# A hybrid encoder layer on one core: mLSTM exponents made from a broadcast row part and a bias column, the row preparation in steps

## The chip, the core and the metric

The kernel runs on one core of a Trainium2 chip. The metric is the device time of one execution in microseconds, compared by medians of several runs. A core has a matrix engine (TensorE, PE in the profile, with PEld for its weight loads), VectorE (DVE), ScalarE (ACT), GpSimd (POOL), and SyncE (SP), which here issues all transfers between the chip's memory and SBUF. Matmul results go to PSUM. Each engine works off its own instructions in order and waits for others by semaphores.

## The reference

The layer takes x (2048 tokens x 1024), 256 memory tokens and the weights. It normalises x and makes one wide projection of it, from which three mixers run: an mLSTM in both directions, an attention in a two-dimensional neighbourhood, and a cross-attention into the memory tokens. Their outputs are projected, weighted by sigmoid gates, summed, projected again and added to x; an MLP with squared ReLU follows. The change touches the mLSTM alone (4 heads, queries and keys of 64, values of 128). Its chunk step in the reference, cut to what matters:

```python
b = jnp.cumsum(lf, axis=-1)
d_log = where(tril, b[..., :, None] - b[..., None, :] + ig[..., None, :], -inf)
inter = b + m_st[..., None]
m_t = maximum(inter, max(d_log, axis=-1))
s = einsum('bhtd,bhsd->bhts', q, k) * exp(d_log - m_t[..., None])
w_inter = exp(inter - m_t)
num = einsum('bhts,bhsv->bhtv', s, v) + w_inter[..., None] * einsum('bhvd,bhtd->bhtv', c_st, q)
den = sum(s, axis=-1) + w_inter * einsum('bhd,bhtd->bht', n_st, q)
h = num / maximum(abs(den), exp(-m_t))[..., None]
```

The exponent of a pair (query t, key s) is a sum of two parts: a_s = ig_s - b_s belongs to the key, r_t = b_t - m_t to the query. In the kernel a tile of exponents has the keys s on the 128 partitions and (head, query t) on the free axis, so that r is the row part and a the column part.

## The kernel before

Three phases follow each other: the projections and the two attentions; the mLSTM, with matmuls of the late gates between its own; then the merge, the output projection and the MLP. Every large product is three fp32r matmuls of split operands, high and low halves (lines L232 to L234). The order on TensorE is written by hand: a generator per stream of work is advanced by one step ("tick") after every six gate matmuls, and what it emits stands there in TensorE's order. The other engines are ordered by a scheduler; for them the place in the program sets the priority.

Phase 2 (`phase_2`) goes from some 950 to 1350 us. `late_gates` gives the 48 groups of 24 gate matmuls with four ticks in each. Its `ml_stream` waits START_2 = 20 ticks and then gives one chunk of 128 tokens per slot of four ticks, forward and backward directions in turn, 32 chunks in all. The table `when` says in which tick of a slot the chunks of the same direction take their next step: an entry (age, ...) is the chunk that began `age` slots of its direction ago.

At the first chunk of each quarter of 512 tokens `ml_block` prepares the rows of its direction: it loads the logs of both gates on four partitions (one a head), scans them to b and m, makes a and r, splits both into halves for an fp32r product (tiles `at` and `rp`), makes w = exp(r + m of the chunk before), stores w, and transposes m by four small matmuls (L773), of which ACT makes exp(-m) (`em`).

`ml_chunk` is the generator of one chunk. Its steps: the loads, and on POOL the tile `rd`, the rows r spread on a block diagonal; then one matmul of `at` and `rd` (L810), which gives a_s + r_t for all heads in PSUM, and the exponential `de` on ACT (L812), masked by POOL; then the scores (L822) or their saved copy `sk`, and `pt` = scores x `de` on DVE; then the transposes of the keys (L839), with `sk` saved by ACT for the direction that passes this chunk later (L832), and the scaled keys `kw`; then the numerator (L863, L866); then the state update (L872, L878), the denominator and `h`. In the later half of a direction's chunks `h` of the other direction (`hf`) is added (L894), squares are summed on ACT (L897), one step later `h` is scaled (L901), and one more step later transposed (L905), split into `hm` and stored. In PSUM this phase has two buffers of 128 x 512 fp32 for the gates (tag mm), four for the numerators (pn), and a ring of two (mx) for everything else, L810 and the transposes included. The gates' results are taken from PSUM by ACT (L600, tile `ev`). A weight comes by DMA as `wr` and is split by ACT (L176) and DVE (L177). `PAD` is the size in bytes of a partition of an unused tile ahead of the tiles of phases 2 and 3 (L251); the large tile X of phase 3 lies behind it.

Of the kernel before, what the change touches and what calls it, by code (L numbers as in the profile page):

```python
# [22 lines left out]
S = 2048  # L23
TB = 512
LOW, LATER, LATER_A, SOON = 100, 60, 60, 40
TICKS_2, START_2 = 4, 20
PAD = 192
EV = {1: 2, 2: 2, 3: 8}
XT = 2
PREP_V = 2  # L30
# [50 lines left out]
class Body:  # L81
# [206 lines left out]
    def scratch(self):  # L288
        d = lambda name, shape, dt=F32: self.p_d.tile(shape, dt, name=name)
        self.scr = dict(  # L290
            qk=d("s_qk", [128, 4, S]),
            v=[d(f"s_v{b}", [TB, 512]) for b in range(NB)],
            og=[d(f"s_o{b}", [TB, 512]) for b in range(NB)],
            gate=[d(f"s_g{b}", [24, 128, TB]) for b in range(NB)],
            qs=d("s_qs", [128, 8, 2, 2, 2, 128]),
            ks=d("s_ks", [128, 2, 2, S]),
            vna=d("s_vna", [2, ROWS, 40, 256]),
            hf=[d(f"s_hf{c}", [128, 512]) for c in range(S // 128)],
            sk=[d(f"s_sk{c}", [128, 6, 128]) for c in range(S // 128)],
            hna=d("s_hna", [128, 2, 2, S]),  # L300
            hmem=d("s_hmem", [128, 2, 2, S]),
            ig=d("s_ig", [8, S]),
            fg=d("s_fg", [8, S]),
            lf=d("s_lf", [8, S]),
            w=[[d(f"s_w{i}{b}", [4, TB]) for b in range(NB)] for i in range(2)],
            hm=[d(f"s_hm{b}", [128, 2, 4, TB]) for b in range(NB)],
            hT={b: d(f"s_hT{b}", [128, 2, 8, TB]) for b in SPILL},
            x2=[d(f"s_x2{b}", [TB, D]) for b in range(NB)],

            a=[[d(f"s_a{i}{q}", [128, 3, 2, TB]) for q in range(FF // 512)] for i in range(NB // 2)],
            s=[[d(f"s_s{i}{q}", [128, 4, 2, TB]) for q in range(FF // 512)] for i in range(NB // 2)],
            t=[d(f"s_t{q}", [128, 2, 2, 2, 512]) for q in range(FF // 512)],
        )
# [308 lines left out]
    def ml_stream(self):  # L624


        for _ in range(START_2):
            yield
        dirs = [list(range(16)), list(range(15, -1, -1))]
        live = [[], []]  # L630
        when = {0: [(2, 0)], 1: [(1, 1), (2, 1), (3, 0)], 2: [(1, 2)], 3: [(3, 0), (1, 3), (0, 1)]}
        d = 0
        while any(dirs) or any(live[0]) or any(live[1]):
            c = dirs[d].pop(0) if dirs[d] else None
            if c is not None and c % 4 == (0, 3)[d]:
# [39 lines left out]
    def ml_consts(self):  # L675
        nc, p = self.nc, self.p_a
        t = lambda name, shape, dt=F32: p.tile(shape, dt, name=name)


        self.reset = t("reset", [36, TB])  # L680
        nc.vector.memset(self.reset, 1.0)
        nc.vector.memset(self.reset.rearrange("p (c t) -> p c t", t=128)[:, :, 0:1], 0.0)

        self.bd = t("bd", [36, 4, 128])
        nc.vector.memset(self.bd, 0.0)
        for d in range(2):
            nc.gpsimd.affine_select(out=self.bd, in_=self.bd, compare_op=ALU.not_equal, fill=1.0, base=-32 * d,
                                    pattern=[[-1, 4], [0, 128]], channel_multiplier=1)


        self.at, self.rd, self.rp = {}, {}, {}
        for d in range(2):
            for i in range(2):
# [3 lines left out]
                for x in (at, rd, rp):  # L697
                    nc.gpsimd.memset(x.bitcast(F32), 0.0)
                for k in range(2):
                    nc.vector.tensor_copy(rd[32 * k:32 * k + 4], self.bd[32 * k:32 * k + 4])  # L700
                    nc.vector.tensor_scalar(at[64 + 32 * k:68 + 32 * k], self.reset[32 * k:32 * k + 4], 0.0, 1.0, ALU.mult, ALU.add)
        self.carry = t("carry", [36, 1])
        nc.vector.memset(self.carry, NEG)
        self.packs = []
# [5 lines left out]
        nc.vector.tensor_scalar(self.gml, raw, 0.5, None, ALU.mult)  # L710
# [27 lines left out]
    def ml_block(self, d, b):  # L738

        nc = self.nc  # L740
        n = b if d == 0 else 3 - b
        hs = slice(32 * d, 32 * d + 4)
        if d == 0:
            self.packs.append({x: self.row("r_" + x, (36, TB + (x == "m")), bufs=1) for x in "ifbmw"})
        P = {x: y[hs] for x, y in self.packs[n].items()}
        ig, lf, bs, m, w = (P[x] for x in "ifbmw")
        nc.sync.dma_start(ig, self.scr["ig"][4 * d:4 * d + 4, b * TB:(b + 1) * TB])
        nc.sync.dma_start(lf, self.scr["lf"][4 * d:4 * d + 4, b * TB:(b + 1) * TB])
        rev = (lambda x: x[:, ::-1]) if d else (lambda x: x)
        nc.vector.tensor_tensor_scan(rev(bs), self.reset[hs], rev(lf), 0.0, ALU.mult, ALU.add)  # L750
        cm, ce = (m[:, 1:], m[:, 0:1]) if d == 0 else (m[:, :TB], m[:, TB:])
        carry = self.carry[hs]
        nc.vector.tensor_copy(ce, carry)
        nc.vector.tensor_tensor_scan(rev(cm), rev(lf), rev(ig), ce, ALU.add, ALU.max)
        nc.vector.tensor_copy(carry, m[:, TB:] if d == 0 else m[:, 0:1])
        lo = slice(32 - 32 * d, 36 - 32 * d)
        at, rp = self.at[d, n % 2], self.rp[d, n % 2]
        a, r = ig, bs
        nc.vector.tensor_tensor(a, ig, bs, ALU.subtract)
        nc.scalar.activation(at[hs], a, AF.Copy)  # L760
        nc.vector.tensor_tensor(at[lo], a, at[hs].bitcast(F32), ALU.subtract)
        nc.vector.tensor_tensor(r, bs, cm, ALU.subtract)
        nc.scalar.activation(rp[hs].bitcast(F32R), r, AF.Copy)
        nc.vector.tensor_tensor(rp[lo], r, rp[hs], ALU.subtract)
        ms = (m[:, 0:TB] if d == 0 else m[:, 1:]).rearrange("p (c t) -> p c t", t=128)
        ms = ms[:, :, 0:1] if d == 0 else ms[:, :, 127:128]
        nc.vector.tensor_tensor(w.rearrange("p (c t) -> p c t", t=128), r.rearrange("p (c t) -> p c t", t=128),
                                ms.to_broadcast([4, 4, 128]), ALU.add)
        nc.scalar.activation(w, w, AF.Exp)
        self.store(self.scr["w"][d][b], w)  # L770
        p = self.ps("mx", (128, 4, 128))
        for c in range(4):
            nc.tensor.transpose(p[:, c, 0:4], cm[:, c * 128:(c + 1) * 128], self.ident[hs, hs])  # L773
        em = self.row(f"r_em{d}", (128, 4, 4))
        nc.scalar.activation(em, p[:, :, 0:4], AF.Exp, scale=-1.0)
        self.rows[d, b] = dict(at=at, rp=rp, em=em)

    def ml_chunk(self, d, c):

# [30 lines left out]
        nc.tensor.matmul(pd, R["at"][:, cs], rd, start=True, stop=True)  # L810
        de = self.t(f"de{d}", [128, 4, 128], 1)
        nc.scalar.activation(de, pd, AF.Exp)  # L812
# [765 lines left out]
```

## Time and profile before

| | |
|---|---|
| median of 3 runs | 2993.33 us (2991.52 to 2995.25) |
| the profiled execution | 2998.03 us, of which the span is 2996.3 us |
| TensorE busy | 2929.4 us, 98% of the span |
| VectorE busy | 2066.5 us, 69% |
| ScalarE busy | 1195.8 us, 40% |
| GpSimd busy | 268.8 us, 9% |
| transfers | 632.97 MB, 211 GB/s on average |

Rows of groups read: line, engine, operation, output<-inputs, count, then the least, median and largest duration in ns or the total in us. Rows of waits read: the waiting engine, its tile and line, "<-", the releaser; then the total in us, how many there were, and the longest. In a stretch of time a row has its length, the busy time of each engine with the number of instructions, the granted clock of TensorE as a share of full speed (PEclk), the busy share of the DMA engines and what they moved. A row of time has start, duration, engine, line, operation and tiles, and in brackets the idle time before it with its releaser.

### The profile page before, as it was taken

The numbers are of one execution on the slowest core, as the hardware profiler recorded it, in microseconds if no ns is written. First come the engines' busy times: TensorE is split into PE (matmuls) and PEld (weight loads), VectorE is DVE, ScalarE is ACT, GpSimd is POOL, SyncE is SP. The second block draws the span as 40 slices with busy tenths as digits, with TensorE's granted clock in tenths as the row PEclk, the third lists the DMA queues.
The fourth block names the chain that finished last, engine by engine and source line by source line (L and its number), as shares of the span: only waits on it lengthen the run. The fifth ranks groups of instructions, "written<-read, shape, count | busy, mean of one in ns | idle before, by whom it ended". The sixth has DMA issues, their size and how long they took to land.

```text
span 2996.3 us, 41916 instructions
## 1 busy us (share of the span) xinstructions
PE 2929.4 (98%) x15028; PEld 2375.1 (79%) x15028; DVE 2066.5 (69%) x3523; ACT 1195.8 (40%) x2198; POOL 268.8 (9%) x423
## 2 busy tenths in 40 slices
PE   8999999999989899999999999999999999999999
PEld 6888888778777677778888888888778888888887
DVE  6676864476654766765688878666675987885665
ACT  6465654355543333342243333533312433334331
POOL 4121200021001323420000000000000000000000
PEclk9999999999999999999999999999999999999999
DMA  8786877876998667788444445766863444466554
GB/s 276 222 275 200 242 231 246 275 215 203 289 283 267 199 202 236 247 275 306 141 132 161 144 149 178 256 195 218 280 209 119 148 151 146 142 223 226 191 185 165
DMA packets 341712, 632.97 MB, mean 211 GB/s; under 512 B 29344, under 2 KB 151008, under 8 KB 341504
## 3 DMA queue, kind: packets, MB, share of 16 engines
q1 hardware_dynamic: 341504, 630.30, 65.5%
q8 instruction: 118, 1.93, 0.3%
q14 instruction: 90, 0.74, 0.1%
HBM read 453.63 MB, written 176.55 MB: 210 GB/s over the span
## 4 chain that ended last, share of the span: by engine, by line
PE 55%; DVE 2%; DMA 2%; issue 1%; ACT 0%; POOL 0%; SPq 0%; DVEq 0%; ACTq 0%; POOLq 0%
PE mm L232 18%; PE mm L233 18%; PE mm L234 18%; PE mm L1341 0%; DMA wr<-in_w_units_dram 0%; DMA hf<-s_hf 0%; DVE h L901 0%; DMA og<-s_o 0%; DVE ev L1497 0%; DVE acc L1490 0%; ACT hf L897 0%; POOL rs L325 0%; DMA X<-s_a 0%; DVE ws L177 0%; DVE h L889 0%
## 5 line engine op out<-in xcount | busy, mean ns | idle before, releaser
L232 PE MATMUL mm<-X,ws 128*128 128x512 f32 x1152 | 455.7, 396 | 0.0
L234 PE MATMUL mm<-X,ws 128*128 128x512 f32 x1152 | 455.4, 395 | 0.0
L233 PE MATMUL mm<-X,ws 128*128 128x512 f32 x1152 | 455.4, 395 | 0.0
L232 PE MATMUL mm<-hT,ws 128*128 128x512 f32 x896 | 375.0, 419 | 8.2 <-DMA hT<-s_hT 4.4
L177 DVE TENSOR_TENSOR ws<-wr,ws 128x1024 fp32r<-128x1024 f32 (+1 forms) x212 | 264.5, 1254 | 136.2 <-ACT ws L176 132.6
L234 PE MATMUL mm<-hT,ws 128*128 128x512 f32 x896 | 353.2, 394 | 0.0
L233 PE MATMUL mm<-hT,ws 128*128 128x512 f32 x896 | 353.2, 394 | 0.0
L233 PE MATMUL mm<-X 128*128 128x512 f32 x896 | 349.6, 390 | 3.4 <-DVE X L1464 3.4
L234 PE MATMUL mm<-X 128*128 128x512 f32 x896 | 349.3, 390 | 0.5 <-DVE X L1464 0.5
L232 PE MATMUL mm<-X 128*128 128x512 f32 x896 | 349.3, 390 | 0.0
L1463 ACT ACTIVATE X<-X 128x1024 fp32r<-128x1024 f32 x176 | 186.6, 1062 | 324.7 <-DMA X<-s_t 115.7
L1464 DVE TENSOR_TENSOR X<-X 128x1024 fp32r<-128x1024 f32 x176 | 214.6, 1224 | 136.7 <-ACT X L1463 135.8
L176 ACT ACTIVATE ws<-wr 128x1024 fp32r<-128x1024 f32 (+1 forms) x212 | 223.4, 1058 | 163.8 <-PE mm L234 88.9
L232 PE MATMUL mm<-ws,hT 128*128 128x512 f32 (+2 forms) x704 | 259.8, 369 | 2.7 <-ACT zif L524 1.8
L234 PEld LDWEIGHTS mm<-X,ws 128*128 128x128 f32 x1152 | 216.4, 188 | 52.3
L232 PEld LDWEIGHTS mm<-X,ws 128*128 128x128 f32 x1152 | 216.4, 188 | 52.2
L233 PEld LDWEIGHTS mm<-X,ws 128*128 128x128 f32 x1152 | 216.5, 188 | 52.1
L234 PE MATMUL mm<-ws,hT 128*128 128x512 f32 (+2 forms) x704 | 249.6, 355 | 2.0 <-DVE hT L434 2.0
L233 PE MATMUL mm<-ws,hT 128*128 128x512 f32 (+2 forms) x704 | 248.9, 354 | 0.0
L202 ACT ACTIVATE ws<-wr 128x512 fp32r<-128x512 f32 x224 | 135.1, 629 | 229.8 <-PE mm L234 148.8
L232 PEld LDWEIGHTS mm<-hT,ws 128*128 128x128 f32 x896 | 170.1, 190 | 49.7 <-issue 10.7
L234 PEld LDWEIGHTS mm<-hT,ws 128*128 128x128 f32 x896 | 169.6, 189 | 38.9
(266 smaller groups left out, 4865.8 us busy)
## 6 DMA issues: line engine op xcount, KB each, us to landing
wr<-in_w_units_dram SPq DMA_DIRECT2D x308, 512.0 KB
s_s<-u SPq DMA_DIRECT2D x32, 1024.0 KB
X<-s_s SPq DMA_DIRECT2D x64, 512.0 KB
X<-s_t SPq DMA_DIRECT2D x64, 512.0 KB
s_g<-ev SPq DMA_DIRECT2D x96, 256.0 KB
ev<-s_g SPq DMA_DIRECT2D x96, 256.0 KB
s_a<-u SPq DMA_DIRECT2D x96, 256.0 KB
X<-s_a SPq DMA_DIRECT2D x48, 512.0 KB
```

The costliest lines, as they stand in the source:

```text
L176: nc.scalar.activation(w[:, 0], raw, AF.Copy)
L177: nc.vector.tensor_tensor(w[:, 1], raw, w[:, 0].bitcast(F32), ALU.subtract)
L202: nc.scalar.activation(hi, src, AF.Copy)
L232: mm(out, lhs[0], rhs[0], start=first, stop=False)
L233: mm(out, lhs[0], rhs[1], start=False, stop=False)
L234: mm(out, lhs[1], rhs[0], start=False, stop=last)
L1463: nc.scalar.activation(hi, src, AF.Copy)
L1464: nc.vector.tensor_tensor(lo, src, hi.bitcast(F32), ALU.subtract)
```

## The change

The tiles `bd`, `at`, `rd`, `rp` and the matmul L810 go. `ml_block` becomes `ml_rows`, a generator for both directions of a block together: one step per tick, with the loads four ticks ahead of the first scan. It stores r to a new scratch `s_r`, and transposes the column part a beside m, giving four bias columns per chunk (`ac`). A chunk loads its 4 x 128 row values to all 128 partitions (`rb`, 256 KB), and `de` is made by four activations, exp(rb + ac), one a head. The first preparation begins at tick 8 of the 20 ahead of the first chunk (ROWS_2), the next ones at slots 3, 11 and 19, that is five slots ahead of their first chunk. One set of row tiles (`pack`) serves all four blocks. In `when` the entry (3, 0) of tick 1 moves to tick 0: in the later half that is the step that scales `h` (L901). PAD goes from 192 to 256 bytes.

```diff
-TICKS_2, START_2 = 4, 20
-PAD = 192
+TICKS_2, START_2, ROWS_2 = 4, 20, 8
+PAD = 256
...
+            r=[[d(f"s_r{i}{b}", [4, 4, 128]) for b in range(NB)] for i in range(2)],
...
-        for _ in range(START_2):
+        rows = self.ml_rows(0)
+        for tick in range(START_2):
+            if tick >= ROWS_2:
+                next(rows, None)
             yield
+        slot = 0
...
-        when = {0: [(2, 0)], 1: [(1, 1), (2, 1), (3, 0)], 2: [(1, 2)], 3: [(3, 0), (1, 3), (0, 1)]}
+        when = {0: [(2, 0), (3, 0)], 1: [(1, 1), (2, 1)], 2: [(1, 2)], 3: [(3, 0), (1, 3), (0, 1)]}
...
-            if c is not None and c % 4 == (0, 3)[d]:
-                self.ml_block(d, c // 4)
+
+            if slot % 8 == 3 and slot < 24:
+                rows = self.ml_rows(slot // 8 + 1)
+            slot += 1
...
+                next(rows, None)
                 yield
...
-        self.bd = t("bd", [36, 4, 128])
...
-                at = self.at[d, i] = t(f"at{d}{i}", [100, TB], F32R)
-                rd = self.rd[d, i] = t(f"rd{d}{i}", [100, 4, 128], F32R)
-                rp = self.rp[d, i] = t(f"rp{d}{i}", [36, TB])
...
+        self.pack = [t("r_" + x, [36, TB + 2 * (x == "m")]) for x in "ifbmw"]
+        for x in self.pack:
+            nc.gpsimd.memset(x, 0.0)
...
+    def ml_rows(self, n):
+        nc = self.nc
+        ig, lf, bs, m, w = self.pack
+        cm, a, r = m[:, 1:TB + 1], ig, bs
+        dirs = [(d, n if d == 0 else 3 - n, slice(32 * d, 32 * d + 4)) for d in range(2)]
+        rev = lambda d, x: x[:, ::-1] if d else x
+        for d, b, hs in dirs:
+            for x, name in ((lf, "lf"), (ig, "ig")):
+                nc.sync.dma_start(x[hs], self.scr[name][4 * d:4 * d + 4, b * TB:(b + 1) * TB])
+        for _ in range(4):
+            yield
+        for d, _, hs in dirs:
+            nc.vector.tensor_tensor_scan(rev(d, bs[hs]), self.reset[hs], rev(d, lf[hs]), 0.0, ALU.mult, ALU.add)
+            yield
+        for d, _, hs in dirs:
+            ce = m[hs, 0:1] if d == 0 else m[hs, TB + 1:TB + 2]
+            carry = self.carry[hs]
+            nc.vector.tensor_copy(ce, carry)
+            nc.vector.tensor_tensor_scan(rev(d, cm[hs]), rev(d, lf[hs]), rev(d, ig[hs]), ce, ALU.add, ALU.max)
+            nc.vector.tensor_copy(carry, m[hs, TB:TB + 1] if d == 0 else m[hs, 1:2])
+            yield
         nc.vector.tensor_tensor(a, ig, bs, ALU.subtract)
...
         nc.vector.tensor_tensor(r, bs, cm, ALU.subtract)
...
+        for d, b, hs in dirs:
+            self.store(self.scr["r"][d][b].rearrange("c h t -> h c t"), r[hs].rearrange("h (c t) -> h c t", t=128))
+        yield
+        for d, _, hs in dirs:
+            ms = (m[hs, 0:TB] if d == 0 else m[hs, 2:TB + 2]).rearrange("p (c t) -> p c t", t=128)
+            ms = ms[:, :, 0:1] if d == 0 else ms[:, :, 127:128]
+            nc.vector.tensor_tensor(w[hs].rearrange("p (c t) -> p c t", t=128), r[hs].rearrange("p (c t) -> p c t", t=128),
+                                    ms.to_broadcast([4, 4, 128]), ALU.add)
         nc.scalar.activation(w, w, AF.Exp)
+        for d, b, hs in dirs:
+            self.store(self.scr["w"][d][b], w[hs])
+        for d, b, hs in dirs:
+            yield
+            p = self.ps("mx", (128, 4, 128))
+            for c in range(4):
+                for x, col in ((cm, 0), (a, 4)):
+                    nc.tensor.transpose(p[:, c, col:col + 4], x[hs, c * 128:(c + 1) * 128], self.ident[hs, hs])
+            em, ac = self.row(f"r_em{d}", (128, 4, 4)), self.row(f"r_a{d}", (128, 4, 4))
+            nc.scalar.activation(em, p[:, :, 0:4], AF.Exp, scale=-1.0)
+            nc.vector.tensor_copy(ac, p[:, :, 4:8])
+            self.rows[d, b] = dict(em=em, ac=ac)
...
-        rd = self.rd[d, c % 2]
+
+        rb = self.t(f"rb{d}", [128, 4, 128], 2)
+        nc.sync.dma_start(rb, self.scr["r"][d][b][cc].unsqueeze(0).to_broadcast([128, 4, 128]))
...
-        nc.gpsimd.tensor_tensor(rd[64:100], self.bd, R["rp"][:, cs].unsqueeze(1).to_broadcast([36, 4, 128]), ALU.mult)
-        yield
-        pd = self.ps("mx", (128, 4, 128))
-        nc.tensor.matmul(pd, R["at"][:, cs], rd, start=True, stop=True)
+        yield
         de = self.t(f"de{d}", [128, 4, 128], 1)
-        nc.scalar.activation(de, pd, AF.Exp)
+        for h in range(4):
+            nc.scalar.activation(de[:, h], rb[:, h], AF.Exp, bias=R["ac"][:, cc, h:h + 1])
```

On TensorE, in the first half of phase 2, a chunk's `at`-`rd` matmul stands between a gate's three matmuls (tile mm) and the state update of the chunk before (L872). Before:

```order
L232 MATMUL mm_11528<-hT,ws_11112 128x512
L233 MATMUL mm_11528<-hT,ws_11112 128x512
L234 MATMUL mm_11528<-hT,ws_11112 128x512
L810 MATMUL mx_11551<-rd_10790,at_10779 128x512
L872 MATMUL mx_11556<-v_2015_11233,kw_2015_11410 64x129 x4
L232 MATMUL mm_11528<-hT,ws_11112 128x512
```

After:

```order
L232 MATMUL mm_11849<-hT,ws_11324 128x512
L233 MATMUL mm_11849<-hT,ws_11324 128x512
L234 MATMUL mm_11849<-hT,ws_11324 128x512
L870 MATMUL mx_11878<-v_2045_11539,kw_2085_11728 64x129 x4
L232 MATMUL mm_11849<-hT,ws_11324 128x512
```

The matmul at L810 is gone and nothing takes its place; the update (L870 now) follows the gate directly, and takes the ring's next buffer.

On VectorE, at the start of phase 2, from the pad to the first instruction of the log-sigmoid (L729 before, L720 after; tiles `ev`). Before:

```order
L251 MEMSET pad_10743 128x48
L681 MEMSET reset 36x512
L685 MEMSET bd 36x512
L682 MEMSET reset 36x4
L703 MEMSET carry 36x1
L701 TENSOR_SCALAR at_10759<-reset 4x512 x2
L701 TENSOR_SCALAR at_10769<-reset 4x512 x2
L701 TENSOR_SCALAR at_10779<-reset 4x512
L700 CAST rd_10760<-bd 4x512 x2
L700 CAST rd_10770<-bd 4x512 x2
L700 CAST rd_10780<-bd 4x512 x2
```

After:

```order
L251 MEMSET pad_10751 128x64
L689 MEMSET reset 36x512
L692 MEMSET carry 36x1
L690 MEMSET reset 36x4
L748 COPY r_m<-carry 4x1 x2
L701 TENSOR_SCALAR gml<-ev_10772 128x512
L720 TENSOR_SCALAR ev_10775<-ev_10775 128x128
```

The 16 conversions of `at` and `rd` (the fence before shows the first 11 of them) stood ahead of the scaling of `gml` and of the log-sigmoid; now those two follow the pad and the constants.

On VectorE, the first row preparation (the scans carry the name SCALAR_TENSOR_TENSOR; r_f, r_i, r_b, r_m and r_w are the two logs, b, m and w). Before:

```order
L750 SCALAR_TENSOR_TENSOR r_b_10996<-reset,r_f_10995 4x512
L754 SCALAR_TENSOR_TENSOR r_m_10997<-r_f_10995,r_m_10997,r_i_10994 4x512
L177 TENSOR_TENSOR ws_10884<-wr_10883,ws_10884 128x8x128
L755 COPY carry<-r_m_10997 4x1
L759 TENSOR_TENSOR r_i_10994<-r_i_10994,r_b_10996 4x512
L750 SCALAR_TENSOR_TENSOR r_b_10996<-reset,r_f_10995 4x512
L762 TENSOR_TENSOR r_b_10996<-r_b_10996,r_m_10997 4x512
L761 TENSOR_TENSOR at_10759<-r_i_10994,at_10759 4x512
L767 TENSOR_TENSOR r_w_10998<-r_b_10996,r_m_10997 4x512
L764 TENSOR_TENSOR rp_10761<-r_b_10996,rp_10761 4x512
```

After:

```order
L743 SCALAR_TENSOR_TENSOR r_b<-reset,r_f 4x512
L749 SCALAR_TENSOR_TENSOR r_m<-r_f,r_m,r_i 4x512
L743 SCALAR_TENSOR_TENSOR r_b<-reset,r_f 4x512
L750 COPY carry<-r_m 4x1
L177 TENSOR_TENSOR ws_10854<-wr_10853,ws_10854 128x8x128
L749 SCALAR_TENSOR_TENSOR r_m<-r_f,r_m,r_i 4x512
L750 COPY carry<-r_m 4x1
L752 TENSOR_TENSOR r_i<-r_i,r_b 36x512
L753 TENSOR_TENSOR r_b<-r_b,r_m 36x512
L760 TENSOR_TENSOR r_w<-r_b,r_m 4x512 x2
```

Both directions' scans now stand together, the two subtractions cover both directions on 36 partitions, and the instructions that split `at` and `rp` (L761, L764) are gone.

More of the change, by code (lines that the diff above doesn't have):

```diff
@@ L682, in ml_consts @@
         nc.vector.memset(self.reset.rearrange("p (c t) -> p c t", t=128)[:, :, 0:1], 0.0)
-        self.bd = t("bd", [36, 4, 128])
[L685 to L693, printed above, removed]
-                at = self.at[d, i] = t(f"at{d}{i}", [100, TB], F32R)
-                rd = self.rd[d, i] = t(f"rd{d}{i}", [100, 4, 128], F32R)
-                rp = self.rp[d, i] = t(f"rp{d}{i}", [36, TB])
[L697 to L701, printed above, removed]
         self.carry = t("carry", [36, 1])
         nc.vector.memset(self.carry, NEG)
-        self.packs = []
+        self.pack = [t("r_" + x, [36, TB + 2 * (x == "m")]) for x in "ifbmw"]
+        for x in self.pack:
+            nc.gpsimd.memset(x, 0.0)
         self.rows = {}
@@ L736, in ml_logsig @@
         self.store(view(self.scr["lf"]), l)
-    def ml_block(self, d, b):
+    def ml_rows(self, n):
         nc = self.nc
[L741 to L758, printed above, removed]
@@ L759, in ml_block @@
+        for d, _, hs in dirs:
[5 more added lines that the diff above has]
+            yield
         nc.vector.tensor_tensor(a, ig, bs, ALU.subtract)
-        nc.scalar.activation(at[hs], a, AF.Copy)
@@ L761, in ml_block @@
-        nc.vector.tensor_tensor(at[lo], a, at[hs].bitcast(F32), ALU.subtract)
         nc.vector.tensor_tensor(r, bs, cm, ALU.subtract)
[L763 to L768, printed above, removed]
@@ L769, in ml_block @@
-        nc.scalar.activation(w, w, AF.Exp)
[L770 to L776, printed above, removed]
+        for d, b, hs in dirs:
+            self.store(self.scr["r"][d][b].rearrange("c h t -> h c t"), r[hs].rearrange("h (c t) -> h c t", t=128))
```

## Prediction

> **What bounds the kernel now.** I read the page first, then the busy time by stretches, then the waits of TensorE alone, and last the order of time around the longest of them.
>
> ```profile
> span 2996.3 us, 41916 instructions
> PE 2929.4 (98%) x15028; PEld 2375.1 (79%) x15028; DVE 2066.5 (69%) x3523; ACT 1195.8 (40%) x2198; POOL 268.8 (9%) x423
> ...
> core 0: us, PE busy (x) PEld busy (x) DVE busy (x) ACT busy (x) POOL busy (x), PEclk, DMA share, GB/s
> 1000.00:1100.00 100.00, 89.09 (x513) 65.61 (x512) 66.70 (x124) 36.91 (x84) 31.62 (x36) 0.97 0.62 202
> 1200.00:1250.00 50.00, 46.68 (x269) 35.26 (x265) 35.99 (x78) 17.45 (x61) 20.11 (x29) 1.00 0.78 241
> 1250.00:1300.00 50.00, 45.66 (x258) 35.01 (x258) 34.31 (x80) 19.80 (x70) 20.36 (x28) 0.97 0.88 270
> 1350.00:1400.00 50.00, 49.99 (x218) 40.80 (x219) 19.80 (x27) 11.09 (x15) 0.00 (x0) 1.00 0.93 342
> ```
>
> TensorE is busy for 98% of the span, so only two things count: TensorE work, and the 67 us in which it stands idle. Idle time of the other engines costs nothing by itself. From 1350 on TensorE has no holes to speak of; in the mLSTM stage (some 950 to 1350 us) it loses 7 to 11% of each of these stretches. These are its waits between 900 and 1400 us, all of them, and one row for the stretch 870 to 1000:
>
> ```profile
> PE mx L839 <- ACT sk L832: 7.4, 3, 5.9
> PE mm L232 <- DMA hT<-s_hT: 4.4, 1, 4.4
> PE mm L232 <- ACT ev L600: 3.8, 3, 1.9
> PE mx L872 <- DVE hm L908: 3.3, 5, 1.0
> PE tr L905 <- ACT de L812: 2.3, 1, 2.3
> PE mx L828 <- DVE kw L845: 2.2, 1, 2.2
> PE mx L828 <- ACT de L812: 2.0, 2, 1.0
> PE mx L828 <- DVE C L878: 1.4, 3, 0.8
> PE mx L810 <- ACT sm L883: 1.1, 1, 1.1
> PE tr L905 <- DVE C L878: 0.7, 1, 0.7
> PE tr L905 <- DVE h L901: 0.3, 1, 0.3
> PE mx L773 <- DVE C L878: 0.2, 1, 0.2
> ...
> PE mm L232 <- ACT ev L600: 3.1, 2, 1.9
> ```
>
> They sum to 29.1 us. The 4.4 us for the reload of hT come before the changed code and stay. Of the 3.8 us for ACT's gate copies 3.1 lie before 1000 us, at the stage's start, and 0.7 later, after the last chunk. So 24.0 us of waits lie in the reach of the change.
>
> **The matmul that goes.** Each of the 32 chunks loses its 100x512 matmul at L810.
>
> ```profile
> L810 PE MATMUL mx<-rd,at x32: 391/400/502, 998.9 to 1310.9; 100*128 100x512 f32 x32
> ...
> 998.63 0.39 PE L234 MATMUL mm<-hT,ws 128*128 128x512 f32 x1
> 998.86 0.39 PE L810 MATMUL mx<-rd,at 100*128 100x512 f32 x1
> 999.09 0.39 PE L232 MATMUL mm<-hT,ws 128*128 128x512 f32 x1
> ...
> 1058.65 0.40 PE L773 MATMUL mx<-ident,r_m 4*128 4x4 f32 x4
> 1058.99 0.71 PE L863 MATMUL pn<-v,pt 128*128 128x129 f32 x4
> ```
>
> A row's duration of 0.39 us overlaps its neighbours; what a matmul costs is the distance between starts: 0.23 us. 32 x 0.23 = 7.4 us less work. In its place each of the eight row preparations (four quarters, two directions) transposes a second set of 4x128 rows, four more small transposes: the four at 1058.65 hold TensorE for 0.34 us, so 8 x 0.34 = 2.7 us more. Bounds: 0 (hidden in the switch) to 2.7; I take the row. Net -4.7 us.
>
> **The exponent.** DVE no longer splits at and rp, POOL no longer builds rd, and ACT makes four 128x128 exponentials with a bias column instead of one 128x512.
>
> ```profile
> L812 ACT ACTIVATE de<-mx x32: 570/598/602, 999.3 to 1311.4; 128x512 f32<-128x512 f32 x32
> L897 ACT ACTIVATE hf<-h x64: 292/295/313, 1189.8 to 1335.6; 128x128 f32<-128x128 f32 x64
> ```
>
> Four at 0.295 us are 1.18 against 0.60 us: 32 x 0.58 = 19 us more ACT time, less the 16 copies of at and rp that go. ACT is at most 40% busy in the stage (19.80 of 50 us above), so this is covered; what counts is that the exponential no longer waits for a TensorE result. It needs the loaded rows and a column that stands ready for four chunks, so it can run before TensorE asks. Uncovered, it would cost at most the 19 us. The Trainium skill speaks against the edit: "ScalarE: Activation LUTs", section "What ACT_TABLE_LOAD costs", puts a pointer-operand bias at some 93 ns per instruction. By that, as an estimate, ACT's addition would be 32 x 4 x 0.093 = 12 us larger, and still under cover; no row here has such a bias on 128 columns to check it.
>
> **The row preparation.** In the kernel before it runs whole, for one direction, at a chunk's start, and DVE and ACT work it off in front of the chunks. The 5.9 us in the first waits row is one such case. Now it runs in steps, one a tick, both directions together, and starts at least five slots ahead (a slot being the four ticks of one chunk). It also leaves the stage's start, where the set-up of at and rd holds DVE:
>
> ```profile
> 953.98 1.65 DVE L701 TENSOR_SCALAR at<-reset 4x512 fp32r<-4x512 f32 x2
> 958.37 3.51 DVE L700 CAST rd<-bd 4x512 fp32r<-4x512 f32 x6
> ...
> 964.53 0.60 ACT L600 ACTIVATE ev<-mm 128x512 f32<-128x512 f32 x1 [4.94 <-DVE gml L710]
> ```
>
> Those conversions fill DVE from 954 to 964 us. Behind them in DVE's queue stands the log-sigmoid, and behind that, on ACT, the first gate copy, for which TensorE waits (part of the 3.1 us). Without them the rows of the first block can be ready some 10 us sooner; as they are now asked for two ticks earlier (transposes in the fifth gate, not at the sixth), this cover is needed. I count the 3.1 us as gained.
>
> What stays: the later three preparations still put four scans and four subtractions or additions into DVE's queue, and a chunk's product pt, on which ACT's copy sk and then the transpose at L839 wait, can stand behind one of them. I keep the waits of this kind whole except the 5.9: 1.5 at L839, 2.0 and 1.4 at L828, together 4.9 us. Bounds: 0 and all 13.0 us of L839 and L828 (7.4 + 2.2 + 2.0 + 1.4). I take 5.
>
> **The output part and the ring.** Without L810 the PSUM ring mx (two buffers) is asked for less: in the later half of the stage a chunk takes two buffers (state update, output transpose) instead of three, so the update no longer meets the buffer that hm has yet to read (3.3 us), and the transposes at L905 and L773 (2.3 + 0.7 + 0.3 + 0.2) and L810 itself (1.1) lose theirs. The scaling of h a tick sooner gives the transposes two ticks more than they need by the 0.3 us row. These 7.9 us go, with bounds of 0 and 7.9. So of 24.0 us 19.0 go.
>
> **The clock.** After two of the waits the granted clock was down:
>
> ```profile
> 1010.00:1020.00 10.00, 4.10 (x20) 3.08 (x19) 9.78 (x12) 3.72 (x8) 5.65 (x3) 0.79 0.22 82
> 1020.00:1030.00 10.00, 10.00 (x52) 7.59 (x52) 8.82 (x19) 4.36 (x10) 3.19 (x4) 0.87 0.62 199
> 1280.00:1290.00 10.00, 7.66 (x38) 5.88 (x36) 5.06 (x12) 3.81 (x14) 3.72 (x6) 0.83 0.93 276
> ```
>
> Lost there: 0.21 x 4.10 + 0.13 x 10 + 0.17 x 7.66 = 3.5 us. Those waits go, so this goes; if they stay, so does this.
>
> **New transfers.** Each chunk loads its rows to all partitions, 256 KB; each preparation stores 2 x 8 KB. On SP's one queue that is some 40 more issues, past which weights, chunk loads and stores move. I count them as covered, with the first rival as price if not. The wider pad shifts every tile of the two later stages by 64 bytes; for that I take 0.
>
> **Sum:** -7.4 + 2.7 - 19.0 - 3.5 = -27.2 us. The profiled execution took 2998.03 us (span 2996.3), 4.7 above the median of 2993.33, so 2970.8 there and **2966** in the median. The likeliest case alone spans 2960 (all waits go) to 2974 (8 us more stay).
>
> **Rivals.**
>
> *The transfers pace the later half.* There each chunk also loads saved products, gates and the other direction's output.
>
> ```profile
> 1277.00 0.43 SPq L172 DMA_DIRECT2D wr<-in_w_units_dram  x1
> 1284.22 1.06 ACT L176 ACTIVATE ws<-wr 128x1024 fp32r<-128x1024 f32 x1 [7.57 <-DMA wr<-in_w_units_dram]
> ```
>
> A weight load took 7 us to arrive and ACT stood 7.57 us for it. The 32 matmuls of L810 span 312 us, 10.1 per chunk; 0.262 MB at the 342 GB/s and 0.93 share of the stretch 1350 to 1400 are 0.7 us of transfer, so 0.88 becomes 0.95 between 1250 and 1300, and a stage shorter by some 8% brings it to 1. Against it: 0.78 in the 50 us before, and loads are issued several ticks ahead. If it holds, the later half keeps its pace: 7.9 of waits, 2.3 of net matmul time and 1.3 of clock, 11.5 us, are not gained: 2978. Chance 0.20.
>
> *The steps still come as a burst.* The DVE order shows the four scans of a preparation close together, and both directions at once. If each of the three later ones costs what the first did, 5.9 + 2.2 of waits and 2.2 of clock, 31 us instead of 5: 2992, and the change would not do what it says. Against it: DVE is two thirds busy, and most steps fall between chunks' own needs. Chance 0.09.
>
> *The rows come late.* The load of a chunk's rows has six ticks, 1.5 slots or 15 us, until the exponential. SP is one queue; if its delay and the landing pass 15 us, ACT stops in front of pt and every chunk of the later half is late.
>
> ```profile
> SPq L797 <- PE mx L839: 30.1, 14, 5.7
> ```
>
> The queue stood up to 5.7 us for one load and 7 us went to landing: 12.7 of 15. At 2.5 us past the mark, 16 chunks cost 40 us: 3006, **slower than before**. Chance 0.06.
>
> *The pad makes phase 3 faster.* After the pad comes X, at byte 96960 of a partition before and 97024 now: 192 and 0 beyond a multiple of 256. TensorE waits for X in phase 3:
>
> ```profile
> PE mm L233 <- DVE X L1464: 3.4, 2, 2.2
> ```
>
> If X's loads got quicker, up to these 3.4 us would go: 2963. Chance 0.07. The Trainium skill, "DMA: Bandwidth & Descriptors", section "How a descriptor splits into AXI transactions", has a transfer that doesn't start on a 256-byte mark pay an extra transaction; whether it holds for SBUF writes no run here shows.
>
> **How the numbers follow.** The forecast has 0.58. Range: down to 2956 (all 24 us of waits and the 3.4 of X, with no cost for the transposes), up to 2986 (the first rival and 8 us of further waits); it leaves out the second and third rival. 0.2%, 6 us, is about what a measurement tells from no change: faster means under 2987.3. That holds for nearly all of the forecast, the first and the last rival: 0.84; same 0.10 (the burst, and a tail of the forecast), slower 0.06.
>
> **What would show it.** Right: no L810, no wait of TensorE over 2 us between 950 and 1340, the clock at 1.00 there, ACT's first gate copy before 962, the last chunk some 27 us earlier, and from the merge on the same durations. Wrong: waits of L837 on sk of several us at the preparations (burst); DMA share at 1 and ACT waiting on weight loads after 1180 (transfers); ACT's exponential waiting on rb (late rows); shorter waits on X after 1380 (pad).

## The result and the profile after

The changed kernel takes 2978.94 us in the median (2973.06 to 2981.19, 4 runs) against 2992.89 us before (2991.52 to 2995.25, 4 runs): 0.995 of the time, interval 0.9932 to 0.9967. That is 14 us less where 27 were forecast; it lies in the range, near the time of the first rival. The stages show that this is not half of the forecast come true. In each profile the same three gate copies on ScalarE serve as marks: one shortly before the mLSTM stage, one in the middle of the mLSTM stage, one after it. Before:

```profile
904.29 0.60 ACT L600 ACTIVATE ev<-mm 128x512 f32<-128x512 f32 x1 [0.90 <-PE mm L234]
...
1174.70 0.58 ACT L600 ACTIVATE ev<-mm 128x512 f32<-128x512 f32 x1
...
1372.10 0.60 ACT L600 ACTIVATE ev<-mm 128x512 f32<-128x512 f32 x1 [3.89 <-PE mm L234]
```

After:

```profile
907.06 0.60 ACT L601 ACTIVATE ev<-mm 128x512 f32<-128x512 f32 x1 [0.90 <-PE mm L234]
...
1163.35 0.58 ACT L601 ACTIVATE ev<-mm 128x512 f32<-128x512 f32 x1
...
1376.46 0.60 ACT L601 ACTIVATE ev<-mm 128x512 f32<-128x512 f32 x1 [3.90 <-PE mm L234]
```

From mark to mark, and from the last one to the end of the span (2996.3 and 2978.0 us):

| stage | before, us | after, us | difference | forecast |
|---|---|---|---|---|
| up to the first mark | 904.3 | 907.1 | +2.8 | 0 |
| first half of the mLSTM | 270.4 | 256.3 | -14.1 | about -16 |
| later half | 197.4 | 213.1 | +15.7 | -11.5 |
| from there on | 1624.2 | 1601.5 | -22.7 | 0 |
| span | 2996.3 | 2978.0 | -18.3 | -27 |

(The forecast's 11.5 for the later half is the amount that its first rival took away, and the first half is the rest. The two profiles differ by 18.3 us, the medians by 14: the profiled execution of before lies 5 us above its median, that of after 1 us.) The mLSTM as a whole gained nothing: what its first half won its later half lost. The time was won in phase 3, whose instructions the change doesn't touch. The part up to the first mark, too, is unchanged work; in the runs of this document it lies between 900.3 and 911.4 us, so differences of a few us between single profiles mean nothing.

TensorE's six longest waits after, between 900 and 1400 us:

```profile
PE tr L903 <- DVE h L899: 8.7, 12, 1.7
PE tr L903 <- DVE sm L884: 6.4, 5, 1.7
PE mm L232 <- DMA hT<-s_hT: 4.3, 2, 2.7
PE mx L826 <- DVE C L876: 3.8, 3, 2.1
PE mx L770 <- ACT sk L830: 2.1, 2, 1.0
PE mx L837 <- ACT sk L830: 1.5, 1, 1.5
```

The 5.9 us at the key transposes and the 3.1 us for the first gate copies are gone, as forecast. In their place stand 15.1 us (8.7 + 6.4) at the output transposes L903 (L905 before), which were to need nothing. The stretches show where, and that TensorE's clock went down there with the waits:

```profile
1100.00:1150.00 50.00, 47.85 (x293) 35.48 (x292) 27.60 (x57) 19.46 (x55) 9.89 (x15) 1.00 0.77 240
1250.00:1300.00 50.00, 44.01 (x226) 31.80 (x225) 30.86 (x71) 20.66 (x79) 12.26 (x22) 0.93 0.86 270
1300.00:1350.00 50.00, 44.19 (x216) 34.15 (x215) 29.73 (x69) 22.74 (x75) 9.10 (x15) 0.97 0.86 268
...
1600.00:1700.00 100.00, 100.00 (x443) 82.80 (x442) 82.06 (x126) 30.82 (x52) 0.00 (x0) 1.00 0.45 156
```

Between 1250 and 1300 us TensorE ran 226 matmuls where before it ran 258 (the row is in the prediction). The last row is the MLP. Before, it read:

```profile
1600.00:1700.00 100.00, 100.00 (x430) 80.55 (x430) 79.51 (x122) 30.65 (x51) 0.00 (x0) 1.00 0.43 151
...
1900.00:2000.00 100.00, 100.00 (x443) 82.81 (x442) 61.89 (x63) 45.55 (x50) 0.00 (x0) 1.00 0.62 203
```

TensorE is without a hole in both, at full clock in both, and yet 430 matmuls of 128x512 fall into these 100 us before and 443 after (a row also counts those that run over its edges). The starts themselves give the distance. Before, then after:

```profile
1640.19 0.39 PE L234 MATMUL mm<-X,ws 128*128 128x512 f32 x1
...
1679.86 0.39 PE L233 MATMUL mm<-X,ws 128*128 128x512 f32 x1
```

```profile
1640.19 0.39 PE L232 MATMUL mm<-X,ws 128*128 128x512 f32 x1
...
1679.86 0.39 PE L233 MATMUL mm<-X,ws 128*128 128x512 f32 x1
```

From the first to the last of these rows 171 matmuls start before and 176 after: one every 233.3 ns against one every 226.7. "Busy" at 100% doesn't say at what rate. The row of 1900 to 2000 us is the down projection, where moving and stationary operand are both in X: there the old kernel, too, ran at 443. Of the slow kind (mm<-X,ws: moving X, stationary ws) there are 3 x 1152 = 3456; 6.6 ns each is 23 us, the whole of phase 3's gain.

### The profile page after: what moved, and what is told of

Same layout as the page of the kernel before. It is cut to its first block, busy times and chain, and to the rows that moved or that the text cites. A ratio compares the mean times of both kernels' runs of the same rounds, so it can differ in the third digit from the quotient of the medians.

```text
span 2978.0 us, 41895 instructions
## 1 busy us (share of the span) xinstructions
PE 2907.8 (98%) x15028; PEld 2374.2 (80%) x15028; DVE 2024.5 (68%) x3490; ACT 1204.6 (40%) x2274; POOL 212.4 (7%) x382
## 4 chain that ended last, share of the span: by engine, by line
PE 56%; DMA 3%; DVE 2%; SPq 1%; issue 1%; ACT 1%; POOL 0%; DVEq 0%; ACTq 0%
PE mm L232 18%; PE mm L234 18%; PE mm L233 18%; DMA wr<-in_w_units_dram 1%; DMA rb<-s_r 1%; PE mm L1339 0%; PE pn L861 0%; SPq L101 0%; DMA s_hm<-hm 0%; DMA hT<-s_hT 0%; PE pn L864 0%; DVE ev L1495 0%; DVE acc L1488 0%; DMA wb<-s_w 0%; DVE h L899 0%
## 5 line engine op out<-in xcount | busy, mean ns | idle before, releaser
L232 PE MATMUL mm<-X,ws 128*128 128x512 f32 x1152 | 448.5, 389 | 0.0
L234 PE MATMUL mm<-X,ws 128*128 128x512 f32 x1152 | 448.2, 389 | 0.0
L233 PE MATMUL mm<-X,ws 128*128 128x512 f32 x1152 | 448.1, 389 | 0.0
```

The costliest lines, as they stand in the source:

```text
L232: mm(out, lhs[0], rhs[0], start=first, stop=False)
L233: mm(out, lhs[0], rhs[1], start=False, stop=False)
L234: mm(out, lhs[1], rhs[0], start=False, stop=last)
```

## The experiments

Two questions were open: what made phase 3 faster, and what made the later half of the mLSTM slower. All times are medians, with ratio and interval against the kernel before, as run beside them (2991 to 2995 us there); the stages are those of one profile each, in us.

| kernel | us | ratio (interval) | first half | later half | after it |
|---|---|---|---|---|---|
| changed kernel | 2978.94 | 0.995 (0.9932 to 0.9967) | 256.3 | 213.1 | 1601.5 |
| before, PAD 256 | 2972.80 | 0.9927 (0.9910 to 0.9944) | 267.6 | 194.0 | 1600.4 |
| changed, PAD 192 | 2997.41 | 1.0016 (1.0005 to 1.0027) | 257.4 | 212.7 | 1621.9 |
| changed, scaling in tick 1 | 2975.51 | 0.9936 (0.9922 to 0.9949) | 253.6 | 211.3 | 1598.5 |
| changed, 2 hm | 2969.37 | 0.9914 (0.9899 to 0.9930) | 257.0 | 203.6 | 1602.6 |
| changed, 2 hm, 2 og | 2953.11 | 0.9868 (0.9846 to 0.9889) | 253.9 | 191.1 | 1599.8 |
| changed, 2 hm, 2 og, 2 hf | 2955.55 | 0.9872 (0.9853 to 0.9892) | 255.8 | 192.7 | 1602.1 |
| changed, rows loaded once | 2943.10 | 0.9823 (0.9796 to 0.9849) | 253.8 | 185.9 | 1604.2 |
| before, one more load | 3004.98 | 1.0041 (1.0028 to 1.0055) | 275.4 | 204.0 | 1623.6 |
| before, ws and X both at 192 | 2967.77 | 0.9921 (0.9908 to 0.9935) | 268.4 | 195.7 | 1602.4 |
| before, PAD 128 | 2987.93 | 0.9988 (0.9979 to 0.9998) | 269.3 | 194.6 | 1621.3 |
| before, PAD 256, 2 hm, 2 og | 2967.46 | 0.9920 (0.9906 to 0.9934) | 267.3 | 189.3 | 1601.4 |
| changed, 2 hm, 2 og, rows late | 2960.39 | 0.9898 (0.9884 to 0.9911) | 252.9 | 205.8 | 1600.5 |

### The pad

```diff
-PAD = 192
+PAD = 256
```

> The kernel before with PAD = 256 and nothing else. Theory A (the place of X in its partition sets the rate of the MLP's matmuls; the trace of the changed kernel has 443 matmuls per 100 us between 1600 and 1800 us where before had 430): the same 443 here, and 17 us less, some 2976 us. Theory B (phase 3 is faster because of what the mLSTM change leaves behind, not because of the pad): 430 matmuls, 2993 us.

Measured: 2972.80 us, 20 us less than before, with this row:

```profile
1600.00:1700.00 100.00, 100.00 (x443) 82.85 (x442) 82.81 (x128) 31.45 (x53) 0.00 (x0) 1.00 0.44 147
```

This one number gives at least as much as the whole change (the two intervals overlap). The other way round:

```diff
-PAD = 256
+PAD = 192
```

> The changed kernel with PAD = 192 again. Theory A: 430 matmuls per 100 us, 17 us more than the changed kernel: 2996 us, so that the mLSTM part alone gains nothing (0 to +3 us against before). Theory B: 443 matmuls and 2979 us.

Measured: 2997.41 us, 0.16% slower than before, at 430 matmuls per 100 us. Theory A holds: the gain was the pad's, and the rest of the change cost some 4 us.

Why the place matters was asked with the old kernel. In it X lies 192 bytes beyond a multiple of 256 and the weights' tiles ws lie on one. Here both were put at 192, X where it had always been:

```diff
-PAD = 192
+PAD = 256
...
-            self.pad(self.p_ws, 128)
+            self.pad(self.p_ws, 64)
```

> The kernel before with X at the same byte 96960 of a partition (192 beyond a multiple of 256) as it had, but with the weights' tiles ws and all that lies between moved 64 bytes down, so that ws, too, lies 192 beyond a multiple of 256 (byte 1216; before at 1280, a multiple). Theory G (what counts is how the moving operand X stands to the stationary operand ws: the stage with both in X ran at 443 matmuls per 100 us with X at 192 as well): 443 matmuls between 1600 and 1800 us, some 2973 us. Theory H (X itself has to lie on a multiple of 256): 430 matmuls, 2993 us.

Measured: 2967.77 us, and the fast rate:

```profile
1600.00:1700.00 100.00, 100.00 (x443) 82.81 (x442) 82.94 (x128) 32.40 (x54) 0.00 (x0) 1.00 0.43 145
```

X itself need not lie on a multiple of 256: theory H falls, and theory G, that how X lies to ws decides, has what it forecast. The tiles between the two were moved along with ws, though. One more distance, with ws on a multiple again:

```diff
-PAD = 192
+PAD = 128
```

> The kernel before with PAD = 128: X 128 beyond a multiple of 256, ws on one. If any place off a multiple of 256 is slow (G and H alike): 430 matmuls per 100 us or fewer, 2993 us or more. If half a step of 256 is as good as a whole one: 443 and 2973 us.

Measured: 2987.93 us and the slow rate:

```profile
1600.00:1700.00 100.00, 100.00 (x432) 81.10 (x431) 79.92 (x123) 31.18 (x52) 0.00 (x0) 1.00 0.44 153
```

So 128 is not as good as 0: in the trace the starts lie 232.4 ns apart, nearly as far as with 192. A distance of 64 was not tried for this group of matmuls.

### The later half

Here is one slot of the changed kernel in order of time, ScalarE, GpSimd, VectorE and SP's queue, from their own rows:

```profile
1252.10 0.60 ACT L905 ACTIVATE hm<-tr 128x512 fp32r<-128x512 f32 x1 [5.66 <-DMA s_hm<-hm]
1252.59 0.30 ACT L895 ACTIVATE hf<-h 128x128 f32<-128x128 f32 x1
...
1254.22 1.01 POOL L326 TENSOR_TENSOR rs<-rs,mhalf 128x4 f32<-128x4 f32 x1
...
1255.27 0.35 DVE L899 SCALAR_TENSOR_TENSOR h<-h,rs,og 128x128 f32<-128x128 f32 x1 [1.10 <-POOL rs L326]
...
1257.54 0.32 SPq L850 DMA_DIRECT2D og<-s_o  x1
1257.96 0.38 SPq L856 DMA_DIRECT2D hf<-s_hf  x1
1258.43 0.93 SPq L101 DMA_DIRECT2D s_hm<-hm  x2
...
1263.80 0.60 ACT L905 ACTIVATE hm<-tr 128x512 fp32r<-128x512 f32 x1 [4.82 <-DMA s_hm<-hm]
```

The copy into `hm` (one buffer) waits until the last chunk's `hm` has been stored. Behind it on ScalarE stand the squares of the next chunk; these give rs, with which VectorE scales `h`; the load of `og` (one buffer per direction) waits in SP's queue until that scaling has read the old `og`; and the store of `hm` stands behind this load in the same queue, followed by the loads of another chunk, `rb` among them. It lands some 5 us later, and the next copy goes. That is a loop over four engines, 1263.80 - 1252.10 = 11.7 us long, where the chunks of the first half come 9.5 us apart. In the kernel before the squares stood ahead of the copy on ScalarE:

```profile
1255.24 0.31 ACT L897 ACTIVATE hf<-h 128x128 f32<-128x128 f32 x1 [3.45 <-DVE h L894]
...
1257.01 0.60 ACT L907 ACTIVATE hm<-tr 128x512 fp32r<-128x512 f32 x1
```

so they did not wait for the store, and the loop was open. Of the first 15 of the 16 copies, 1 stood ahead of the next chunk's squares before, and 9 do in the changed kernel. The waits of ScalarE in the later half (1180 to 1345 us) say the same. After, then before:

```profile
ACT hm L905 <- DMA s_hm<-hm: 37.1, 9, 5.7
ACT de L810 <- DMA rb<-s_r: 18.9, 10, 3.0
```

```profile
ACT hm L907 <- DMA s_hm<-hm: 2.8, 3, 1.2
```

The first test gives the copy a second buffer:

```diff
-        hm = self.t("hm", [128, 2, 4, 128], 1, F32R)
+        hm = self.t("hm", [128, 2, 4, 128], 2, F32R)
```

> The changed kernel with two buffers for hm (4 KB more per partition). Theory C (a loop over three engines sets the slot in the later half: ACT's copy hm waits for the store of the one before; behind it on ACT stand the squares of the next chunk, then rs, the scaling, the og load that waits for the scaling on SP's queue, and behind that the store): ACT's 37.1 us of waits for the store of hm and TensorE's 15.1 us of waits at the output transposes go, and with them most of the 20 us that the later half lost: 2959 to 2965 us. Theory D (the 256 KB of rb per chunk are too much for the transfers): the waits move to rb and to weight loads, not under 2972 us.

Measured: 2969.37 us, the waits for the store gone, 9.5 us of the later half back, half of what theory C said. ScalarE now waited 26.2 us for the rows `rb`. What was left, on SP's queue and on TensorE:

```profile
SPq L850 <- DVE h L899: 38.0, 12, 4.7
...
PE tr L903 <- DVE h L899: 6.7, 12, 0.8
PE tr L903 <- DVE sm L884: 3.6, 3, 1.7
```

The tick of the scaling, taken back:

```diff
-        when = {0: [(2, 0), (3, 0)], 1: [(1, 1), (2, 1)], 2: [(1, 2)], 3: [(3, 0), (1, 3), (0, 1)]}
+        when = {0: [(2, 0)], 1: [(1, 1), (2, 1), (3, 0)], 2: [(1, 2)], 3: [(3, 0), (1, 3), (0, 1)]}
```

> The changed kernel with the outputs scaled in tick 1 again. Theory E (scaling a tick sooner is what put the squares behind hm on ACT, or what makes the og load collide): the later half gets its 20 us back, 2959 to 2965 us. Theory C or D: ACT's order of hm and squares is not set by this tick, 2979 us within 4.

Measured: 2975.51 us, its interval overlapping that of the changed kernel; ScalarE still waits 32.3 us for the store and the later half takes 211.3 us. Theory E falls as a cause of the later half's loss. Whether the tick is worth a us or two, these runs don't tell.

Then the queue, with a second buffer for `og` beside that for `hm`:

```diff
-            og = self.t(f"og{d}", [128, 512], 1)
+            og = self.t(f"og{d}", [128, 512], 2)
```

> The changed kernel with two buffers each for hm and og. With hm alone (2969 us) SP's queue still stood 38 us at the og load, until the scaling had read the og before, and hf, hm stores, chunk loads and rb stood behind it. Theory C (what is left is that queue): the 38 us go, the loads of rb land sooner, ACT's 26 us of waits for rb go, and the later half takes 194 to 197 us instead of 204: 2960 to 2963 us. Theory D (the transfers themselves are too many): rb and weight loads are waited for as before, 2969 us.

Measured: 2953.11 us, better than expected; the later half takes 191.1 us.

```profile
PE tr L903 <- DVE h L899: 2.4, 7, 0.6
...
1200.00:1250.00 50.00, 49.66 (x293) 37.80 (x292) 35.15 (x80) 23.13 (x85) 12.53 (x24) 1.00 1.02 330
```

The output transposes wait 2.4 us instead of 15.1. The transfers now run at 330 GB/s with the DMA share at its top in this stretch, so it was not the number of bytes that had held the slots back: they had been kept from starting. This is the fastest kernel here that computes everything, 1.3% under the one before. A second buffer for `hf` as well:

```diff
-            hf = self.t(f"hf{d}", [128, 4, 128], 1)
+            hf = self.t(f"hf{d}", [128, 4, 128], 2)
```

> As the kernel with two buffers for hm and og, and two for hf as well, so that the load of the other direction's output waits for nothing in use either. Theory C: 2957 to 2963 us, with ACT's 30 us of waits for the sum of h and hf down to half. Theory D: 2969 us, the transfers only start sooner and share the same rate.

Measured: 2955.55 us, no further gain. With the queue free VectorE had waited only 0.8 us for `hf` between 1180 and 1345 us, so there was little to win.

Next, what closed the loop. Here the rows are loaded at the first chunk of a direction only:

```diff
+        self.rb = [None, None]
...
-        rb = self.t(f"rb{d}", [128, 4, 128], 2)
-        nc.sync.dma_start(rb, self.scr["r"][d][b][cc].unsqueeze(0).to_broadcast([128, 4, 128]))
+        if first:
+            self.rb[d] = self.p_a.tile([128, 4, 128], F32, name=f"rb{d}")
+            nc.sync.dma_start(self.rb[d], self.scr["r"][d][b][cc].unsqueeze(0).to_broadcast([128, 4, 128]))
+        rb = self.rb[d]
```

> The changed kernel with the rows rb loaded once per direction instead of once per chunk; it leaves the rows of all later chunks out, which are computed with those of the first. Theory F (the 32 loads of 256 KB are what made the later half slow, by the transfers or by what they put in front of the store of hm): the later half back to 195 to 198 us, 2963 us. If the loop of theory C needs no rb: 211 us, 2979 us.

Measured: 2943.10 us, 20 us below what theory F said, and a later half of 185.9 us, with ScalarE's wait for the store at 6.1 us although `hm` has one buffer. And the load alone, put into the kernel before:

```diff
         rd = self.rd[d, c % 2]
+        xb = self.t(f"xb{d}", [128, 4, 128], 2)
+        nc.sync.dma_start(xb, self.scr["v"][b][cs].rearrange("t (h e) -> t h e", h=4))
```

> The kernel before (PAD = 192) with one more load of 256 KB per chunk, into a tile that nothing reads, at the place where the changed kernel loads rb. Theory F: the later half grows from 197 to some 212 us, 3008 us against 2993. If the load costs only where something waits for it: 2993 to 2997 us.

Measured: 3004.98 us, 10 us more, though nothing reads what it loads. In the profiles the later half is 6.6 us longer, where theory F said 15, and the first half 5.0 us. ScalarE's waits for the store of `hm` grow from 2.8 to

```profile
ACT hm L909 <- DMA s_hm<-hm: 11.9, 3, 6.2
```

So theory F holds in its direction, and in neither size: without the loads of the rows the loop hardly closes, but one more load of the same size in the old kernel makes less than half of the loss. The order that the scheduler gave to ScalarE goes with the loads: the copy stands ahead of the next squares in 9 of 15 chunks in the changed kernel, in 1 without the loads of the rows, and in 4 with the added load in the old kernel. With two buffers each for `hm` and `og` it stands so in 10, and the later half takes 191.1 us all the same: this order costs little where the copy need not wait. What of the loss is the order and what the length of the queue was not taken apart.

### What the mLSTM change is worth without the loop

The same two buffers and the pad of 256 in the kernel before:

> The kernel before with PAD = 256 and two buffers each for hm and og: the mLSTM without the change, but with the buffers that the changed one was short of. If the row part and the steps are worth what the first half shows (254 to 257 us against 268 to 270): a first half of 268, a later half of 190, 2964 to 2970 us against 2953. If the changed kernel has nothing over it once the buffers are there: 2953 to 2957 us.

Measured: 2967.46 us, 14 us above the changed kernel with the same buffers (0.9920, 0.9906 to 0.9934, against 0.9868, 0.9846 to 0.9889). The first half makes the difference: 267.3 against 253.9 us. TensorE's four longest waits between 900 and 1400 us here:

```profile
PE mx L839 <- ACT sk L832: 7.4, 3, 5.9
PE mm L232 <- DMA hT<-s_hT: 2.8, 1, 2.8
PE mx L828 <- ACT de L812: 2.2, 2, 1.1
PE mm L232 <- ACT ev L600: 2.1, 2, 1.3
```

The last experiment takes the head start of the row preparation away and leaves the rest:

```diff
-            if slot % 8 == 3 and slot < 24:
-                rows = self.ml_rows(slot // 8 + 1)
+            if slot % 8 == 0 and slot < 32:
+                for _ in self.ml_rows(slot // 8):
+                    pass
```

(and no steps during START_2 or behind the chunks' ticks).

> The changed kernel with two buffers for hm and og (2953 us), but the row preparation of both directions whole at the first chunk of a block, as the kernel before does it, instead of five slots ahead. If the head start is what won the first half: TensorE waits 5 us or more at each of the four preparations, first half back to 264 to 268 us, 2965 to 2975 us. If the smaller DVE work alone won it: 254 to 257 us, 2953 to 2956 us.

Measured: 2960.39 us, 7 us more (the two intervals just touch), and not where it was expected. The first half is as short as with the head start; the cost falls on the later half, on one preparation, the one at 1194 us:

```profile
PE mx L767 <- DVE r_m L746: 13.1, 1, 13.1
PE mx L767 <- DVE r_i L749: 3.1, 1, 3.1
...
1200.00:1250.00 50.00, 39.76 (x219) 30.70 (x220) 31.40 (x71) 16.73 (x61) 13.82 (x18) 0.80 0.69 214
```

TensorE stands at the transposes of this preparation from 1194 us on, while three of the four loads of its logs leave SP's queue only from 1200.8 us on. So the head start counts at that one preparation, and the first half was won by the rest: the matmul that went, the conversions that no longer stand at the start, and a preparation with less work. How much each of these won was not measured. The wait of 5.9 us at L839 is gone even without the head start. Before, VectorE stood 5.56 us for the load of one direction's logs, with the product `pt` of a chunk behind the scan:

```profile
1008.20 1.21 DVE L750 TENSOR_TENSOR_SCAN r_b<-reset,r_f 4x512 f32<-4x512 f32 x1 [5.56 <-DMA r_f<-s_lf]
```

In the late version both directions' loads are issued together a slot ahead of where the second was; that this alone removes the wait was not tried.

## Why the prediction came out in range, and where it was wrong

- **The time** lies in the range for the wrong reasons. The later half was 27 us worse than forecast (+15.7 instead of -11.5) and phase 3 was 22.7 us better than the 0 that was taken. Two errors of opposite sign nearly cancelled, and that is luck: in the profiles 18.3 of the 27 us were left.
- **The matmul that goes, the stage's start, the row preparation** (first half): right in size. About 16 us were forecast and 14.1 measured (13.4 in the pair with the same buffers): TensorE's idle time there fell by 9.2 us (20.5 to 11.3) and its busy time by 4.9 us (249.9 to 245.0). The reason given for the 5.9 us was not right: the late version has neither the steps nor the head start, and has lost them too. (The first preparation, moreover, starts 12 ticks ahead of its first chunk, which is three slots and not five.) Which of the rest removed them, the smaller work on VectorE or the earlier loads, stays open.
- **The exponent**: one size and one claim fail. An exponential with a bias column takes 0.389 us, not 0.295, but on ScalarE, too, a row's duration overlaps its neighbours: four in a row take 1.28 us, not 4 x 0.389.

```profile
L810 ACT ACTIVATE de<-rb,r_a x128: 384/389/413, 985.2 to 1313.3; 128x128 f32<-128x128 f32 x128
...
1255.20 1.28 ACT L810 ACTIVATE de<-rb,r_a 128x128 f32<-128x128 f32 x4 [1.22 <-DMA rb<-s_r]
...
L810 ACT ACTIVATE de<-rb,r_a 128x128 f32<-128x128 f32 x128 | 43.0, 393 | 35.3 <-DMA rb<-s_r 21.6 <-issue 12.1 <-POOL v L797 1.5
```

  The group keeps ScalarE busy for 43.0 us, where the one before took 32 x 0.598 = 19.1: 24 us more instead of 19, within its cover all the same. The 94 ns between the two rows agree with the 93 ns that the Trainium skill gives for a pointer operand ("ScalarE: Activation LUTs", "What ACT_TABLE_LOAD costs"). The estimate that the prediction made by it came to 31 us in all; with the overlap it is 24. And "it can run before TensorE asks" held in the first half, but for one wait of 2.7 us; in the later half it waited 18.9 us for `rb`.
- **The output part and the ring**: the step of the sum that failed. It followed the PSUM ring, where the 3.3 us did go, and gave the transposes two ticks more than they need. It didn't follow the SBUF buffers that the output passes, `hm` and `og`, nor what stands behind their waits on ScalarE and on SP's queue. 7.9 us were to go; 15.1 us came at L903.
- **The clock**: right in the first half, where the 2.2 us of its loss went with the waits; in the later half the new waits took it down to 0.93. There it cost again: with fewer instructions (1019 against 1026) TensorE was busy for 195.5 us instead of 188.8, beside 9.0 us more of idle time, and the two make up the 15.7.
- **The first rival** (transfers pace the later half) came nearest in mechanism and, by chance, in time. Its argument against itself, that loads are issued several ticks ahead, was the error: in one queue a load is issued when the one ahead of it no longer waits, and SP's queue stood 40.6 us at the load of `og`. Its price was a gain forgone, not the loss that the loop made. Its cause, a full DMA share, was not it either: the share stood at 0.86, ScalarE waited 17.1 us for weights where it had waited 37.9 us before, and with the two buffers the same bytes went through.
- **The burst**: it didn't come. Of the waits that it would have multiplied, 7.4 us stayed (3.8 at L826, 2.1 at L770, 1.5 at L837), against 5 that the forecast kept. **The rows late**: ScalarE did stop in front of them, 10 times and up to 3.0 us, but with the queue free (two buffers for `hm` and `og`) it waited only 1.6 us for them there.
- **The pad**: taken at 0, with a chance of 0.07 for a gain by shorter waits on X, 3.4 us at most. These waits are the same after:

```profile
L233 PE MATMUL mm<-X 128*128 128x512 f32 x896 | 349.5, 390 | 3.5 <-DVE X L1462 3.5
```

  The gain came from the rate of the matmuls, which the prediction took as fixed. It had looked at X's place for the sake of transfers, beside the rule of the Trainium skill by which a transfer that doesn't start on a 256-byte mark also fetches bytes that it doesn't use ("DMA: Bandwidth & Descriptors", "How a descriptor splits into AXI transactions"). That was not the cause: one run has X at 192 as ever and the fast rate. The trace of before held the hint: the two kinds of MLP matmul, of one shape, at 430 and 443 per 100 us, at full clock and without a wait.

## What to carry to other kernels

Compare the rate of equal matmuls between stages, not only whether TensorE is busy; where one stage is some per cent slower at the same clock, try another place for its tiles. When a load is added, follow the queue that it joins: what waits at its head, which stores stand behind it, and whether an engine's in-order queue closes that chain to a loop. A change of several parts is timed part by part: here one constant carried the whole gain and hid that the rest, as it stood, cost some 4 us, and was worth 14 once two buffers were doubled.

## What the hardware showed that was not expected

fp32r matmuls of 128x512 whose moving operand X lay 192 or 128 bytes (modulo 256) from the place of their stationary operand ws started 233.3 and 232.4 ns apart (430 and 432 in the rows of 100 us); with both at the same place modulo 256, be it 0 or 192, 226.7 ns (443). The clock was 1.00 and TensorE without a wait in all four. By 3456 such matmuls this is 23 us of a profile; the medians fell by 20 us (both at 0) and 23 us (both at 192). What in the reading of the two operands makes the difference no run here shows; in the run with both at 192 not ws alone was moved but all tiles between it and X.
